# Scattering experts' results to rows of token choices, and spreading half of them by one-hot products

## The chip, the cores and the metric

One Trainium2 chip, one core. The metric is the device time of one execution in microseconds, median of the runs. TensorE is called PE, VectorE DVE, ScalarE ACT, GpSimd POOL, SyncE SP.

## What is computed

Two transformer blocks on 512 tokens of width 1024, float32 in and out. Block 1 is attention with a short convolution and an FFN of width 4096. Block 2 is a mixer and a mixture of experts (MoE), and a final norm follows. The change lies in the MoE and, with one step, in the FFN of block 1.

```python
def hierarchical_moe(h, ...):
    grp = argmax(softmax(hf @ w_group + b_group))            # 4 groups of 8 experts
    top_p, top_e = top_k(softmax(logits of the group), 2)    # two experts a token
    weights = p_grp * top_p / sum(top_p)
    ...                                                      # 1024 assignments, sorted by expert
    a = silu(xb @ w_gate[e]) * (xb @ w_up[e])                # 1024 -> 256
    out = (a @ w_down[e]) * weight                           # 256 -> 1024
    y = zeros(T, D).at[slot_tok].add(out)
x = x + gate2 * y;  return rms_norm(x, final_norm_g)
```

## The kernel before, in words

The MoE runs as 17 jobs (`Pair`), one behind the other. Jobs of pairs 0 to 15 hold two experts each with 64 slots for tokens an expert, 128 slots in all; job `NP` (16) is the overflow pair, two blocks of 64 slots for tokens that found no place, whose experts are known only at run time (`xi`). Jobs run in the order 0 to 14, `NP`, 15. A job has these steps:

- six weight panels of 1 MB (two each of gate, up, down; tile `pw`) are loaded on SP's queue into a ring of 17 places (`place`); those of `NP` are gathered on POOL's queue by `xi`;
- `gather`: an indirect DMA on POOL's queue brings the rows of up to 128 tokens from `h2d` by the table `tab` into `xg`;
- `turn`: eight transposes by PE make `xT`;
- `up` (L1898 by way of `both`): 32 pairs of products into two PSUM banks, ACT's silu and DVE's `a` (L1911);
- `turn_a`: two transposes make `aT`;
- `product` (L1898 too): 8 pairs of products of 512 columns; `scaled` (L1929) takes the two halves out of PSUM into `o`;
- `down` (L1938): POOL's queue writes all 128 rows of `o` to rows of the DRAM buffer `ye`, empty slots too.

The last job's result stays on chip: a one-hot matrix `oh` of its slots against the tokens spreads it by products (L1465). For all others, eight indirect gathers (L1490, `results`) bring for each token the two rows of `ye` that belong to it (`src`); the order of what follows is written out by hand in `TAIL`: adding the two rows (DVE L1446, POOL L1444), the residual `x` through PSUM by products with the identity (L1460), the sum (L1451), square, power, scaling (L1483) and the output. A row of zeros in `ye`, written in the FFN of block 1 (L525), serves tokens without a row.

The order of instructions on each engine is otherwise set when the kernel is built: a scheduler places each step by the estimated time at which its inputs are ready, and each engine runs its list in order. `T` is 512, `D` 1024, `P` 128, `NT` 4 tiles of tokens, `CAP` 64.

Of the kernel before, what the change touches and what calls it, by code (L numbers as in the profile page):

```python
# [29 lines left out]
YE = 30  # L30
ZERO = (YE + SX) * CAP
# [10 lines left out]
XGS = 4  # L42
# [4 lines left out]
TPOOL = (0,)  # L47
YPOOL = (1, 2)
YX = (1, 2)
XPE = (0, 1, 2, 3)  # L50
FCUT = [[slice(0, D)]] * 3 + [[slice(0, 512), slice(512, D)]]

TAIL = "d b0 b1 a0 a1 s k e0 e1 a2 t0 t1 b2 e2 b3 e3 t2 a3 f0 t3 f1 f2 f3".split()
# [13 lines left out]
def shape_constants():  # L67
# [27 lines left out]
        it(8) % 4 * P + i[:, None] - float(T),  # L95
# [9 lines left out]
class Emit:  # L105
# [410 lines left out]
    def ffn(self, x1, hh, hl, first, CH=8):  # L516
# [739 lines left out]
    def route_loads(self, mod, op):  # L1256
# [7 lines left out]
        widths = (4, 8, 32, P, 8, NX, 1, XT)  # L1264
# [76 lines left out]
    def moe(self):  # L1341
# [3 lines left out]
        with ExitStack() as c0:  # L1345
# [13 lines left out]
            with self.pool("r1", 1) as r1:  # L1359
                rest = self.route(r1, rp, tab, src, W, xb, nx, sc, kept, ws)  # L1360
            self.banks(t="y", u="zw", d="x")
            with ExitStack() as c1:
                ep = c1.enter_context(self.pool("ep", 1))
                XG = list(self.XG)

                order = list(range(NP - 1)) + [NP, NP - 1]
                jobs = [Pair(self, ep, XG[i % XGS], tab, c) for i, c in enumerate(order)]
# [7 lines left out]
                gf = self.xp.tile([P, D], F32, tag="B2", name="gf")  # L1375
                for i, j in enumerate(jobs):
                    if i > 0:
                        jobs[i - 1].turn_a()
                    if i + 1 < n:
                        jobs[i + 1].turn()  # L1380
                    if i + XGS < n:
                        jobs[i + XGS].gather()
                    if i == n - 3:

                        g1 = self.xp.tile([P, D], F32, tag="xg1", name="gf1")
                        nc.sync.dma_start(g1[0:1, :], I["final_norm_g_2"].unsqueeze(0))
                    if i == n - 2:
                        for half in range(2):
                            hs = slice(half * 512, half * 512 + 512)
                            b = self.bank("d")  # L1390
                            nc.tensor.matmul(b, self.ones[0:1, :], g1[0:1, hs], start=True, stop=True)
                            nc.scalar.copy(gf[:, hs], b)
                        oh = ep.tile([P, T], F32R, tag="oh", name="oh")
                        for tt in range(NT):
                            nc.vector.tensor_scalar(oh[:, tt * P:(tt + 1) * P], self.rt[3], kept, -float(tt * P), op0=ALU.subtract, op1=ALU.is_equal)
# [4 lines left out]
                for tt in range(NT):  # L1400
                    self.results(ys[tt], self.ye, ZERO, src[:, 0], tt)
                self.banks(t="y", u="z", d="wx")
                jobs[-1].turn_a()
                steps = self.combine(x, ys, gf, oh, jobs[-1])
                for c, f in zip("dsk", jobs[-1].last_steps(self.pin, [self.xp.tile([P, D], F32R, tag=f"xg{i}", name=self.nm("k")) for i in (2, 1)])):
                    steps[c] = f
                for c in TAIL:
                    steps[c[0]](*(int(i) for i in c[1:]))
# [4 lines left out]
                with self.tc.If(more > SX):  # L1413
                    self.yx = self.dram.tile([(NX - SX) * CAP, D], F32, tag="yx", name="yx")
                    for c in range(NP + SX // 2, NP + NX // 2):
                        xg = self.place()
                        nc.vector.memset(xg, 0.0)
                        job = Pair(self, ep, xg[:, :D], tab, c)
# [5 lines left out]
                    for tt in range(NT):  # L1424
                        y = self.wr.tile([P, 2, D], F32, tag="wr", name=self.nm("y"))
                        nc.vector.memset(y, 0.0)
                        self.results(y, self.yx, (NX - SX) * CAP - 1, src[:, 1], tt)
                        for k in range(2):
                            nc.vector.tensor_tensor(x[:, tt, :], y[:, k, :], x[:, tt, :], op=ALU.add)
                        self.finish(x, y, gf, tt, ())  # L1430
# [4 lines left out]
    def combine(self, x, ys, gf, oh, last):  # L1435

        nc, pin = self.nc, self.pin
        banks = {}
        halves = (slice(0, 512), slice(512, D))

        def add(tt):
            y = ys[tt]
            if tt in YPOOL:
                nc.gpsimd.tensor_tensor(y[:, 0, :], y[:, 0, :], y[:, 1, :], op=ALU.add)  # L1444
            else:
                pin(nc.vector.tensor_tensor(y[:, 0, :], y[:, 0, :], y[:, 1, :], op=ALU.add))  # L1446

        def total(tt):
            for half, hs in enumerate(halves):
                y = ys[tt][:, 0, hs] if tt in XPE else x[:, tt, hs]  # L1450
                pin(nc.vector.tensor_tensor(x[:, tt, hs], banks[tt, half], y, op=ALU.add))  # L1451

        def onto(tt):
            pin(nc.vector.tensor_tensor(x[:, tt, :], ys[tt][:, 0, :], x[:, tt, :], op=ALU.add))

        def begin(tt):
            for half, hs in enumerate(halves):
                b = banks[tt, half] = self.bank("tu"[half] if tt in YX else "d")
                if tt in XPE:
                    nc.tensor.matmul(b, self.ident, x[:, tt, hs], start=True, stop=False)  # L1460

        def end(tt):
            for half, hs in enumerate(halves):
                for p in range(2):
                    nc.tensor.matmul(banks[tt, half], oh[:, tt * P:(tt + 1) * P], last.kept[p][:, hs], start=tt not in XPE and p == 0, stop=p == 1)  # L1465

        return {"a": add, "t": total, "x": onto, "b": begin, "e": end,
                "f": lambda tt: self.finish(x, ys[tt], gf, tt, TPOOL, pin)}

    def finish(self, x, y, gf, tt, pool, pin=lambda i: i):  # L1470

        nc = self.nc
        xt, y = x[:, tt, :], y[:, 0, :]
        ss = self.sm.tile([P, 2], F32, tag="ss2", name=self.nm("ss"))
        nc.scalar.activation(y, xt, AF.Square, accum_out=ss[:, 0:1])
        self.rsqrt(ss[:, 1:2], ss[:, 0:1], D, 1)
        if tt in pool:
            nc.scalar.activation(y, xt, AF.Copy, scale=ss[:, 1:2])
            nc.gpsimd.tensor_tensor(y, y, gf, op=ALU.mult)
            nc.sync.dma_start(self.out[0, tt * P:(tt + 1) * P, :], y)  # L1480
        else:
            for c in FCUT[tt]:
                pin(nc.vector.scalar_tensor_tensor(y[:, c], xt[:, c], ss[:, 1:2], gf[:, c], op0=ALU.mult, op1=ALU.mult))  # L1483
                nc.sync.dma_start(self.out[0, tt * P:(tt + 1) * P, c], y[:, c])

    def results(self, y, rows, bound, src, tt):

        for k in range(2):
            i = 4 * k + tt
            self.nc.gpsimd.indirect_dma_start(out=y[:, k, :], out_offset=None, in_=rows[:, :], bounds_check=bound, oob_is_err=False,  # L1490
                                              in_offset=bass.IndirectOffsetOnAxis(ap=src[:, i:i + 1], axis=0))

    def route(self, r1, rp, tab, src, W, xb, nx, sc, kept, ws):
        nc, I = self.nc, self.I
        d4, d8, i32, iP, tokv, jx, ip, thr = self.rt
# [72 lines left out]
        def table(vr, w, o, role="b"):  # L1568
# [4 lines left out]
            return tb, beside(o, tb[C, 0:w], lambda o, v: V.tensor_scalar(o, v, float(T), None, op0=ALU.add))  # L1573
# [10 lines left out]
        tb, last = table(vm, 32, tab[:, 0:NP])  # L1584
# [4 lines left out]
        with self.tc.issue_after(last.ins):  # L1589
            beside(kept, tb[C, YE:32], lambda o, v: V.tensor_scalar(o, v, float(T), None, op0=ALU.add))  # L1590
            V.tensor_copy(cum, b[:, 0:160])

        def rest(room, room2):
# [11 lines left out]
            for o, v in ((ei, row(i32, 8)), (xi, row(xb, 8))):  # L1605
# [70 lines left out]
    def place(self):  # L1676
# [299 lines left out]
```

## Time and profile before

| what | value |
|---|---|
| median of 3 runs | 1562.48 us (1559.33 to 1566.56) |
| the profiled execution: its time, its span | 1559.03 us, 1557.1 us |
| PE busy | 1453.4 us, 93% of the span |
| DVE, ACT, POOL busy | 861.1, 568.7, 207.5 us |
| mean granted PE clock | 0.972 of full |
| last `up` ends, last DVE instruction ends | 1510.56, 1543.33 us |

Times in the trace are microseconds from the span's start. The MoE's jobs lie between 1230 and 1511 us. A wait is read in brackets behind an instruction: how long its engine had been idle, and what released it.

### The profile page before, as it was taken

How to read it: one execution, taken by the hardware profiler on the slowest of the kernel's cores; microseconds unless marked ns; L12 is line 12 of the kernel's file. 1: busy time of each engine (PE TensorE's matmuls, PEld its weight loads, DVE VectorE, ACT ScalarE, POOL GpSimd, SP SyncE). 2: the span in 40 equal slices, each digit the busy share in tenths (PEclk: the TensorE clock that was granted, in tenths of full speed). 3: DMA queues.
4: the chain of work that ended last, by engine and by line, in shares of the span. 5: the costliest groups of instructions: out<-in, count | busy, mean ns of one | idle time of the engine just before them, and what ended most of it. 6: DMA issues, size and time to landing. Idle time of an engine off the chain costs nothing.

```text
span 1557.1 us, 20093 instructions
## 1 busy us (share of the span) xinstructions
PE 1453.4 (93%) x7630; PEld 1143.4 (73%) x7630; DVE 861.1 (55%) x1836; ACT 568.7 (37%) x1198; POOL 207.5 (13%) x242
## 2 busy tenths in 40 slices
PE   7999999999999999999999999999999789887882
PEld 6877778798888888887888888888887655554441
DVE  5675887878667664468766342248756731111114
ACT  4444775743332423345443342236622211000101
POOL 2110230111011010030000110000022311010104
PEclk8999999999999999999999999999999889999996
DMA  5325102037555644433322333421167689999964
GB/s 188 101 66 179 73 28 95 1 111 242 187 167 193 210 162 135 139 120 110 109 82 55 99 127 115 135 95 55 54 212 303 265 318 414 425 425 425 426 268 163
DMA packets 131357, 275.46 MB, mean 177 GB/s; under 512 B 17870, under 2 KB 77295, under 8 KB 118200
## 3 DMA queue, kind: packets, MB, share of 16 engines
q1 hardware_dynamic: 117098, 237.66, 42.6%
q0 software_dynamic: 10704, 33.65, 5.7%
q10 hardware_dynamic: 3454, 2.82, 0.6%
q8 instruction: 62, 1.02, 0.3%
q14 instruction: 39, 0.32, 0.1%
HBM read 259.90 MB, written 18.92 MB: 179 GB/s over the span
## 4 chain that ended last, share of the span: by engine, by line
PE 64%; DMA 13%; DVE 5%; issue 5%; ACT 2%; POOL 1%; ACTq 0%; DVEq 0%; POOLq 0%; SPq 0%
PE b L157 18%; PE b L158 18%; PE b L159 18%; DMA pw<-w_expert_up 4%; DMA pw<-w_expert_down 4%; PE b L1898 3%; DMA pw<-w_expert_gate 3%; PE b L218 2%; PE b L821 1%; PE b L822 1%; DMA xg<-h2d,tab 1%; PE b L764 1%; DVE wl L151 1%; PE b L765 1%; DMA wr<-w_out 0%
## 5 line engine op out<-in xcount | busy, mean ns | idle before, releaser
L149 ACT ACTIVATE wh<-wr 128x512 fp32r<-128x512 f32 x361 | 205.3, 622 | 302.3 <-PE b L158 146.3
L151 DVE TENSOR_TENSOR wl<-wr,wh 128x512 fp32r<-128x512 f32 x349 | 235.9, 713 | 143.3 <-ACT wh L149 130.1
L1898 PE MATMUL b<-pw,xT 128*64 128x256 f32 x1088 | 139.0, 395 | 26.9 <-DMA pw<-w_expert_up 14.1
L1898 PEld LDWEIGHTS b<-pw,xT 128*64 128x64 f32 x1088 | 86.3, 141 | 76.5 <-DMA pw<-w_expert_up 17.8
L159 PE MATMUL b<-h2h,wl 128*128 128x512 f32 (+1 forms) x320 | 121.9, 381 | 0.0
L158 PE MATMUL b<-h2l,wh 128*128 128x512 f32 (+1 forms) x320 | 121.9, 381 | 0.0
L157 PE MATMUL b<-h2h,wh 128*128 128x512 f32 (+1 forms) x320 | 121.7, 381 | 0.0
L158 PE MATMUL b<-fl,wh 128*128 128x512 f32 (+1 forms) x288 | 105.2, 366 | 0.0
L157 PE MATMUL b<-fh,wh 128*128 128x512 f32 (+1 forms) x288 | 104.9, 366 | 0.2 <-ACT fh L203 0.2
L159 PE MATMUL b<-fh,wl 128*128 128x512 f32 (+1 forms) x288 | 105.1, 365 | 0.0
L157 PE MATMUL b<-wh,uh 128*128 128x512 f32 x256 | 100.0, 391 | 0.0
L159 PE MATMUL b<-wh,ul 128*128 128x512 f32 x256 | 99.7, 390 | 0.0
L158 PE MATMUL b<-wl,uh 128*128 128x512 f32 x256 | 99.6, 389 | 0.0
L498 DVE SCALAR_TENSOR_TENSOR acc<-wr,cond,acc 128x512 f32<-128x512 f32 x84 | 62.9, 748 | 36.1 <-DMA wr<-mod_w 34.4
L1911 DVE SCALAR_TENSOR_TENSOR a<-b,ws,a 128x256 f32<-128x256 f32 x17 | 8.2, 484 | 126.3 <-PE b L1898 126.3
L159 PEld LDWEIGHTS b<-h2h,wl 128*128 128x128 f32 x320 | 60.6, 189 | 11.4
L158 PEld LDWEIGHTS b<-h2l,wh 128*128 128x128 f32 x320 | 60.5, 189 | 11.3
L157 PEld LDWEIGHTS b<-h2h,wh 128*128 128x128 f32 x320 | 60.5, 190 | 11.2
L1898 PE MATMUL b<-pw,aT 128*64 128x512 f32 x272 | 67.4, 597 | 0.3 <-DMA pw<-w_expert_down 0.3
L157 PEld LDWEIGHTS b<-fh,wh 128*128 128x128 f32 x288 | 54.1, 189 | 9.7 <-ACT fh L203 0.5
L159 PEld LDWEIGHTS b<-fh,wl 128*128 128x128 f32 x288 | 54.3, 189 | 8.9
L158 PEld LDWEIGHTS b<-fl,wh 128*128 128x128 f32 x288 | 54.3, 189 | 8.8 <-DVE fl L204 0.2
(586 smaller groups left out, 3205.8 us busy)
## 6 DMA issues: line engine op xcount, KB each, us to landing
wr<-w_in SPq DMA_DIRECT2D x33, 1024.0 KB
pw<-w_expert_gate SPq DMA_DIRECT2D x32, 1024.0 KB
pw<-w_expert_up SPq DMA_DIRECT2D x32, 1024.0 KB
pw<-w_expert_down SPq DMA_DIRECT2D x32, 1024.0 KB
wr<-mod_w SPq DMA_DIRECT2D x24, 1024.0 KB
wr<-w_up SPq DMA_DIRECT2D x16, 1024.0 KB
wr<-w_down SPq DMA_DIRECT2D x16, 1024.0 KB
ye<-o POOLq DMA_DIRECT2D x16, 512.0 KB, 8.0
```

The costliest lines, as they stand in the source:

```text
L149: nc.scalar.activation(hi[:, c], raw[:, c], AF.Copy)
L151: (nc.gpsimd if i in pool else eng or nc.vector).tensor_tensor(lo[:, c], raw[:, c], hi.bitcast(F32)[:, c], op=ALU.subtract)
L157: mm(o, lh, rh, start=first, stop=False)
L158: mm(o, lh, rl, start=False, stop=False)
L159: mm(o, ll, rh, start=False, stop=last)
L218: self.nc.tensor.transpose(o, i, self.ident[:k, :k])
L498: nc.vector.scalar_tensor_tensor(acc, rv[:, k, :], self.cond[:, kk:kk + 1], acc, op0=ALU.mult, op1=ALU.add)
L764: nc.tensor.matmul(b[:, :n], QS[:, h, qs], KH[:, kind, g, :n], start=True, stop=False)
L765: nc.tensor.matmul(b[:, :n], QS[:, h, qs], KL[:, kind, g, :n], start=False, stop=True)
L821: nc.tensor.matmul(o, v, ph, start=kind == 2, stop=False)
L822: nc.tensor.matmul(o, v, pl, start=False, stop=kind == 1 and kb == qb)
L1898: self.nc.tensor.matmul(o[h, :], x[:, k, h], w[s](k), start=k == ks[0], stop=k == ks[-1])
```

## The change

Eight pairs (`HOT`: 4, 6, 8, 10, 12, 13, 14, 15) no longer write to DRAM. Their `o` is split into a high and a low part (`split`: ACT copies it to fp32r, DVE subtracts), and `spread` adds it to `x`: for each of four token tiles and two halves, two one-hot products of 128x512 into a bank of `c` and a DVE add of 128x512 onto `x`. These steps are given to a later `up` as `fill`, and stand between its products. The last two jobs (pairs 14 and 15) are added in `tail` instead, in PSUM, on top of `ident` times `x`.

The other nine ("cold") jobs write by an indirect DMA: `ye` now has a row for each token and choice (1024 rows), the table `to` says which row a slot goes to, and empty slots lie out of bounds and are not moved. Rows that no slot writes must read as zero or be skipped: four DMAs on SP's queue fill `ye` with zeros in the FFN (1 MB each), and the tile of a gather of results is set to zero first (`memset`).

The order of jobs is now 0 to 11, `NP`, 12, 13, 14, 15. All cold results are then in DRAM four jobs ahead of the end, and the gathers and adds of results stand in jobs 14 and 15 (counted from 0 in the new order), two token tiles each; DVE does all adds, two of 128x1024 a tile. `XGS` falls from 4 to 2: the buffers freed hold high and low parts. The banks of `up` fall from four to two (role `u`), `c` takes the other two. The hand-written `TAIL` order is gone; `finish` reads the sum from PSUM in halves. The routing table has two more small DVE operations ahead of the first gather.

```diff
+HOT = (4, 6, 8, 10, 12, 13, 14, 15)
+ORDER = [*range(12), NP, *range(12, NP)]
-XGS = 4
+XGS = 2
-TAIL = "d b0 b1 a0 a1 s k e0 e1 a2 t0 t1 b2 e2 b3 e3 t2 a3 f0 t3 f1 f2 f3".split()
...
-        self.ye = self.dram.tile([ZERO + 1, D], F32, tag="ye", name="ye")
-        zero = fp.tile([1, D], F32, tag="zero", name="zero")
+        self.ye = self.dram.tile([2 * T, D], F32, tag="ye", name="ye")
+        zero = fp.tile([P, 256], F32, tag="zero", name="zero")
         nc.gpsimd.memset(zero, 0.0)
-        nc.gpsimd.dma_start(self.ye[ZERO:, :], zero)
+        for i in range(4):
+            nc.sync.dma_start(self.ye[i * 256:(i + 1) * 256, :].rearrange("(p a) (b c) -> p (a b) c", p=P, c=256), zero.unsqueeze(1).to_broadcast([P, 8, 256]))
...
-            self.banks(t="y", u="zw", d="x")
+            self.banks(t="y", u="z", c="w", d="x")
...
-                    j.up()
-                    if i > 0:
-                        jobs[i - 1].down()
-                ys = [self.place().rearrange("p (k c) -> p k c", k=2) for _ in range(NT)]
-                for tt in range(NT):
-                    self.results(ys[tt], self.ye, ZERO, src[:, 0], tt)
...
+                    if i == n - 1:
+                        jobs[i - 1].down(kept)
+                    j.up(jobs[i - 2].spread(x) if hot(i - 2) else ())
+                    for tt in (2 * (i - back), 2 * (i - back) + 1):
+
+                        if 0 <= tt < NT:
+                            y = self.place().rearrange("p (k c) -> p k c", k=2)
+                            self.results(y, src[:, 0], tt)
+                            for k in range(2):
+                                nc.vector.tensor_tensor(x[:, tt, :], y[:, k, :], x[:, tt, :], op=ALU.add)
+                    if 0 < i < n - 1:
+                        jobs[i - 1].down(kept)
+                assert hot(n - 1) and hot(n - 2) and back + 1 < n
+                self.tail(x, gf, *jobs[-2:], kept)
...
+    def tail(self, x, gf, prev, last, kept):
...
+        def begin(tt, half, role):
+            b = banks[tt, half] = self.bank(role)
+            nc.tensor.matmul(b, self.ident, x[:, tt, half * 512:half * 512 + 512], start=True, stop=False)
+            prev.onto(b, tt, half, False, False)
...
+        for half in range(2):
+            for tt in range(NT):
+                last.onto(banks[tt, half], tt, half, False, True)
...
-    def results(self, y, rows, bound, src, tt):
-
+    def results(self, y, src, tt):
+
+        self.nc.vector.memset(y, 0.0)
         for k in range(2):
...
-    def down(self):
+    def down(self, kept=None):
         em = self.em
+        if kept is not None and self.c in HOT:
+            self.hot(kept)
+            for i in range(2):
+                self.scaled(self.o, i, self.product(i))
+                self.split(i)
+            return
...
-        self.nc.gpsimd.dma_start(rows[i * P:(i + 1) * P, :], o)
+        self.nc.gpsimd.indirect_dma_start(out=em.ye[:, :], out_offset=bass.IndirectOffsetOnAxis(ap=self.to[:, c:c + 1], axis=0),
+                                          in_=o, in_offset=None, bounds_check=2 * T - 1, oob_is_err=False)
...
+    def onto(self, b, tt, half, first, last):
+
+        for i, k in enumerate((self.hi, self.lo)):
+            self.nc.tensor.matmul(b, self.oh[:, tt * P:(tt + 1) * P], k[:, half * 512:half * 512 + 512], start=first and i == 0, stop=last and i == 1)
+
+    def spread(self, x):
+
+        def step(tt, half):
+            b = self.em.bank("c")
+            self.onto(b, tt, half, True, True)
+            xs = x[:, tt, half * 512:half * 512 + 512]
+            self.nc.vector.tensor_tensor(xs, b, xs, op=ALU.add)
+
+        return [lambda tt=tt, half=half: step(tt, half) for half in range(2) for tt in range(NT)]
```

Three places of the order show what moved. SP's queue at the start of the FFN of block 1, before (`wr` is a panel of weights; L492 serves the modulation of block 2, whose work is spread over the FFN):

```order
L492 DMA wr_3653<-mod_w 128x4x512
L138 DMA wr_3659<-w_up 128x8x256
L492 DMA wr_3731<-mod_w 128x4x512
L138 DMA wr_3741<-w_up 128x8x256
L492 DMA wr_3816<-mod_w 128x4x512
L492 DMA wr_3831<-mod_w 128x4x512
L138 DMA wr_3841<-w_down 128x4x512
```

and of the change:

```order
L486 DMA wr_3656<-mod_w 128x4x512
L132 DMA wr_3662<-w_up 128x8x256
L520 DMA ye<-zero 1024x1x256 x4
L486 DMA wr_3734<-mod_w 128x4x512
L132 DMA wr_3744<-w_up 128x8x256
L486 DMA wr_3819<-mod_w 128x4x512
L486 DMA wr_3834<-mod_w 128x4x512
L132 DMA wr_3844<-w_down 128x4x512
```

The four DMAs that write zeros stand ahead of two panels of the modulation and one of the FFN, and panels behind them keep their order.

POOL's queue through the last jobs, before (`xi` rows are the overflow pair's panels, `ye<-o` a job's result, `pw<-ye,src` a gather of results):

```order
L1938 DMA ye<-o_12207 128x1024
L1693 DMA pw_12258<-w_expert_up,xi 128x2048
L1693 DMA pw_12262<-w_expert_up,xi 128x2048
L1693 DMA pw_12266<-w_expert_down,xi 128x2048
L1693 DMA pw_12270<-w_expert_down,xi 128x2048
L1938 DMA ye<-o_12311 128x1024
L1938 DMA ye<-o_12379 128x1024
L1490 DMA pw_12393<-ye,src 128x1024 x2
```

and of the change, where `ye<-o_12017` is pair 9's result, `ye<-o_12241` pair 11's and `ye<-o_12327` the overflow pair's:

```order
L1932 DMA ye<-o_12017,to 1024x1024
L1864 DMA xg_10017<-h2d,tab 128x1024
L1679 DMA pw_12160<-w_expert_up,xi 128x2048
L1679 DMA pw_12164<-w_expert_down,xi 128x2048
L1679 DMA pw_12148<-w_expert_gate,xi 128x2048
L1679 DMA pw_12168<-w_expert_down,xi 128x2048
L1932 DMA ye<-o_12241,to 1024x1024
L1864 DMA xg_10018<-h2d,tab 128x1024
L1864 DMA xg_10017<-h2d,tab 128x1024
L1932 DMA ye<-o_12327,to 1024x1024
L1475 DMA pw_12425<-ye,src 128x1024 x2
L1475 DMA pw_12574<-ye,src 128x1024 x2
```

The overflow pair's panels now stand two cold results ahead of its own, and the gathers of results stand behind that last scatter with nothing else in between, two for each token tile (those of the last two tiles follow).

DVE's list of the change in jobs 13 to 15 (`a_12412` is `a` of job 14, `a_12561` of job 15; `o_12435` and `k_12437` are pair 12's result and its low part, `o_12584` and `k_12586` pair 13's; `x<-pw` adds a gathered row onto `x`, `x<-b` a spread):

```order
L1472 MEMSET pw_12425 128x2048
L1918 TENSOR_TENSOR o_12435<-b_12443,S_10003 128x512
L198 TENSOR_TENSOR k_12437<-o_12435,k_12436 128x512
L1397 TENSOR_TENSOR x_10000<-pw_12425,x_10000 128x1024
L1918 TENSOR_TENSOR o_12435<-b_12451,S_10003 128x512
L1397 TENSOR_TENSOR x_10000<-pw_12425,x_10000 128x1024
L198 TENSOR_TENSOR k_12437<-o_12435,k_12436 128x512
L1472 MEMSET pw_12574 128x2048
L1472 MEMSET pw_12415 128x2048
L1900 SCALAR_TENSOR_TENSOR a_12412<-b_12395,ws,a_12412 128x256
L1963 TENSOR_TENSOR x_10000<-b_12506,x_10000 128x512
L1877 COPY xT_12464<-b_12471 128x512
```

and further on, at job 15:

```order
L198 TENSOR_TENSOR k_12586<-o_12584,k_12585 128x512
L1397 TENSOR_TENSOR x_10000<-pw_12574,x_10000 128x1024
L1472 MEMSET pw_12564 128x2048
L1900 SCALAR_TENSOR_TENSOR a_12561<-b_12528,ws,a_12561 128x256
L1397 TENSOR_TENSOR x_10000<-pw_12574,x_10000 128x1024
L1918 TENSOR_TENSOR o_12584<-b_12600,S_10003 128x512
L1946 TENSOR_SCALAR oh_12615<-rt,kept 128x128 x4
L198 TENSOR_TENSOR k_12586<-o_12584,k_12585 128x512
L1397 TENSOR_TENSOR x_10000<-pw_12564,x_10000 128x1024
L1918 TENSOR_TENSOR o_12613<-b_12620,S_10003 128x512
```

In before, none of this stood between `o` and `a`: all adds of gathered rows came behind the last `a`. Now the two adds of the first token tile and the memsets for the next two stand ahead of `a` of job 14, and the adds and memset of later tiles on both sides of `a` of job 15.

## Rows read from the trace of the kernel before

**Rows 1.** The page: busy time of PE; GB/s in 40 slices of the span.

```profile
PE 1453.4 (93%) x7630; PEld 1143.4 (73%) x7630; DVE 861.1 (55%) x1836; ACT 568.7 (37%) x1198; POOL 207.5 (13%) x242
...
GB/s 188 101 66 179 73 28 95 1 111 242 187 167 193 210 162 135 139 120 110 109 82 55 99 127 115 135 95 55 54 212 303 265 318 414 425 425 425 426 268 163
```

**Rows 2.** Stretches of the MoE: us, busy by engine (x), PEclk, DMA share, GB/s.

```profile
1270.00:1340.00 70.00, 69.69 (x519) 40.84 (x516) 14.17 (x22) 7.08 (x16) 9.17 (x12) 1.00 1.01 408
1340.00:1490.00 150.00, 116.98 (x766) 67.52 (x763) 20.94 (x33) 12.28 (x27) 15.87 (x19) 0.96 1.01 425
```

**Rows 3.** Timeline of DVE, 1265 to 1512, ends of `up`: start, us, operation.

```profile
1312.43 0.48 DVE L1911 SCALAR_TENSOR_TENSOR a<-b,ws,a 128x256 f32<-128x256 f32 x1 [6.45 <-PE b L1898]
...
1324.59 0.48 DVE L1911 SCALAR_TENSOR_TENSOR a<-b,ws,a 128x256 f32<-128x256 f32 x1 [6.45 <-PE b L1898]
...
1441.04 0.48 DVE L1911 SCALAR_TENSOR_TENSOR a<-b,ws,a 128x256 f32<-128x256 f32 x1 [8.68 <-PE b L1898]
...
1463.06 0.48 DVE L1911 SCALAR_TENSOR_TENSOR a<-b,ws,a 128x256 f32<-128x256 f32 x1 [13.19 <-PE b L1898]
...
1510.56 0.48 DVE L1911 SCALAR_TENSOR_TENSOR a<-b,ws,a 128x256 f32<-128x256 f32 x1 [3.26 <-PE b L1898]
```

**Rows 4.** Timeline of all engines, 1459 to 1474: one job's turns and product.

```profile
1463.60 0.51 PE L218 MATMUL b<-ident,a 128*128 128x128 f32 x2 [0.65 <-DVE a L1911]
...
1464.20 0.37 ACT L1920 COPY aT<-b 128x256 f32<-128x256 f32 x1 [7.01 <-PE b L218]
...
1465.27 3.70 PE L1898 MATMUL b<-pw,aT 128*64 128x512 f32 x16
```

**Rows 5.** Timeline of all engines, 343 to 349 (FFN).

```profile
343.31 0.37 SPq L138 DMA_DIRECT2D wr<-w_up  x1
...
348.54 0.63 ACT L149 ACTIVATE wh<-wr 128x512 fp32r<-128x512 f32 x1 [1.92 <-DMA wr<-w_up]
```

**Rows 6.** Stretches of the FFN, columns as in rows 2.

```profile
350.00:360.00 10.00, 10.00 (x45) 8.28 (x45) 8.50 (x13) 3.60 (x7) 1.07 (x1) 1.00 0.77 257
370.00:400.00 30.00, 30.00 (x133) 24.37 (x133) 20.75 (x32) 7.18 (x14) 2.78 (x4) 1.00 0.66 215
```

**Rows 7.** Groups of 1180 to 1557: busy us, mean ns, idle before.

```profile
L1451 DVE TENSOR_TENSOR x<-b,pw 128x512 f32<-128x512 f32 x8 | 5.1, 685 | 2.1 <-PE b L1465 2.0
...
L1951 DVE TENSOR_TENSOR k<-o,k 128x512 fp32r<-128x512 f32 x2 | 1.3, 688 | 0.1
```

**Rows 8.** Timeline of all engines, 1469 to 1492: panels of the overflow pair.

```profile
1470.90 1.04 POOL L1693 DMA_INDIRECT pw<-w_expert_up,xi  x1 [0.34 <-PE b L1391]
...
1489.11 1.12 PE L1898 MATMUL b<-pw,xT 128*64 128x256 f32 x4 [4.22 <-DMA pw<-w_expert_up,xi]
```

**Rows 9.** Timeline of all engines, 1500 to 1545: the tail.

```profile
1512.81 0.55 POOL L1938 DMA_DIRECT2D ye<-o  x1 [12.02 <-DVE o L1929]
...
1516.59 3.70 PE L1460 MATMUL b<-x,ident 128*128 128x512 f32 x8
1516.60 1.03 POOL L1490 DMA_INDIRECT pw<-ye,src  x1 [3.24 <-DMA ye<-o]
...
1517.94 1.03 POOL L1490 DMA_INDIRECT pw<-ye,src  x1 [0.30 <-issue]
...
1523.29 1.23 DVE L1446 TENSOR_TENSOR pw<-pw 128x1024 f32<-128x1024 f32 x1 [10.78 <-DMA pw<-ye,src]
1524.43 1.28 DVE L1929 TENSOR_TENSOR o<-b,S 128x512 f32<-128x512 f32 x2
...
1540.72 2.61 DVE L1483 SCALAR_TENSOR_TENSOR pw<-x,ss,gf 128x1024 f32<-128x1024 f32 x3 [0.55 <-POOL ss L214]
```

**Rows 10.** DMA issues of 1230 to 1557: KB each, median us to landing.

```profile
ye<-o POOLq DMA_DIRECT2D x16, 512.0 KB, 8.0
...
pw<-ye,src POOLq DMA_INDIRECT x8, 6.4
```

More of the change, by code (lines that the diff above doesn't have):

```diff
@@ L1375, in moe @@
                 gf = self.xp.tile([P, D], F32, tag="B2", name="gf")
+                hot = lambda i: i >= 0 and jobs[i].c in HOT
+                back = max(i for i in range(n) if not hot(i)) + 2
                 for i, j in enumerate(jobs):
@@ L1432, in pin @@
     def pin(self, i):
         return self.tc.keep_in_program_order(i)
-    def combine(self, x, ys, gf, oh, last):
-        nc, pin = self.nc, self.pin
+    def tail(self, x, gf, prev, last, kept):
+        nc = self.nc
         banks = {}
[L1439 to L1468, printed above, removed]
@@ L1486, in results @@
-    def results(self, y, rows, bound, src, tt):
+        def begin(tt, half, role):
+            b = banks[tt, half] = self.bank(role)
+            nc.tensor.matmul(b, self.ident, x[:, tt, half * 512:half * 512 + 512], start=True, stop=False)
+            prev.onto(b, tt, half, False, False)
+        last.turn_a()
+        for tt, role in ((0, "c"), (1, "u")):
+            for half in range(2):
+                begin(tt, half, role)
+        products = [last.product(i) for i in range(2)]
+        for half in range(2):
+            begin(2, half, "t")
@@ new lines, in tail @@
+        last.hot(kept)
+        for half in range(2):
+            last.scaled(last.o, half, products[half])
+            last.split(half)
+        for half in range(2):
+            begin(3, half, "d")
+        for half in range(2):
+            for tt in range(NT):
+                last.onto(banks[tt, half], tt, half, False, True)
+        for tt in range(NT):
+            self.finish(gf, tt, [banks[tt, half] for half in range(2)], self.place()[:, :D])
+        for tt, half in sorted(banks):
+            nc.scalar.copy(x[:, tt, half * 512:half * 512 + 512], banks[tt, half])
@@ L1583, in route @@
             tt_(oc[:, hs], row(iC, 4), bc(pos[:, hs], CAP), ALU.is_equal)
-        tb, last = table(vm, 32, tab[:, 0:NP])
+        rows, last = table(vm, 32, slice(0, NP))
         warm = self.bank()
@@ new lines, in hot @@
+    def hot(self, kept):
+        em, nc = self.em, self.nc
+        self.o = self.tl("o", D)
+        if self.c in ORDER[-2:]:
+            k = em.place(F32R)
+            self.hi, self.lo = k[:, :D], k[:, D:]
+        else:
+            self.hi, self.lo = (em.xp.tile([P, D], F32R, tag=f"xg{i}", name=em.nm("k")) for i in (2, 3))
+        self.oh = self.tl("oh", T, dt=F32R)
+        for tt in range(NT):
+            nc.vector.tensor_scalar(self.oh[:, tt * P:(tt + 1) * P], em.rt[3], kept[:, self.c:self.c + 1], -float(tt * P), op0=ALU.subtract, op1=ALU.is_equal)
```

145 lines of the change are left out of this document (58 added, 87 removed).

## Prediction

> **What bounds the kernel now.** I read the page first, then stretches, then single jobs. The page [rows 1] has PE busy for 93% of the span, which is an average over two regimes: the GB/s line climbs to 425 and stays there for the last fifth. The stretches [rows 2] divide that fifth. From 1270 to 1340 us PE is busy 69.69 of 70 us, so PE sets the pace although the DMA engines are full too. From 1340 to 1490 PE is busy 116.98 of 150 and the DMA share is 1.01 at 425 GB/s: weight panels set the pace. The reader is to see a prefetch that is used up by 1340. The end of each `up` [rows 3] gives the pace of a job: 12.16 us (1312.43 to 1324.59) where PE is the bound, (1441.04 − 1324.59)/7 = 16.6 us where panels are. The last `up` ends at 1510.56, the last DVE instruction at 1543.33, the span at 1557.1: 13.8 us of output and closing lie behind it. The profiled run took 1559.03 us, 3.45 below the median of the three, 1562.48. My sum is made against 1557.1 and 3.45 + 1.93 is added to it.
>
> **One job, in prices.** In [rows 4], counted from DVE's `a` at 1463.06 [rows 3]: `turn_a` and `turn` run 1463.60 to 1465.27, the product 3.70 more, to 1468.97. That leaves 12.16 − 1.67 − 3.70 = 6.79 us for `up`. Where the product stands ahead of the next `up`, PE can do nothing while `a` and its transposed copy (0.37) are made, and a job takes 5.91 + 0.37 + 6.79 = 13.1 us.
>
> **What the change does, part by part.**
>
> *Bytes.* Sixteen writes of 512 KB go, 8.39 MB, of which fourteen (7.3 MB) were issued while the DMA engines were full. Nine scatters take their place. Counting the fixed inputs' routing, pairs 0, 1, 2, 3, 5, 7, 9 and 11 hold 444 filled slots and the two overflow blocks 41; 485 rows of 4 KB are 1.99 MB. The gathers of results (again 1.99 MB, empty sources are skipped) move from the free DMA engines at the end into the full stretch. That is 7.3 − 4.0 = 3.3 MB less, at 425 GB/s 7.8 us of panel time.
>
> *Zeroing.* Four DMAs of 1 MB write zeros on SP's ring at the start of the FFN, ahead of a mod_w and of the w_up issued at 343.31 [rows 5]. From 350 to 360 the engines moved 257 GB/s at share 0.77 [rows 6], 334 GB/s at share 1, so 4.19 MB take 12.6 us, from about 333 to 346. ACT already waited 1.92 us for that w_up, until 348.54; it will land near 354.5 and the w_down behind it is late too. PE was full (10.00 of 10, 30.00 of 30) on what had been prepared. Between nothing (all of the 6 us absorbed) and 10 us (two panels late, nothing absorbed) I take 5 us, lost by PE. The two further DVE operations in the routing table ahead of the first gather cost 0.4 us.
>
> *Hot pairs on PE.* Each of eight adds 16 products of 128x512 in fp32r. In the FFN 133 of that shape took 30 us of a full PE [rows 6], 0.226 each, so 3.63 us. The low part of the result (0.69 [rows 7]; ACT makes the high part beside it) is ahead of the first of them, and the eight adds of DVE, 0.685 each [rows 7], follow over two banks, in groups of four: 0.7 for the split and about 2 us of bank waits. I take 6.4 us where a spread lies inside an `up`, bounds 3.6 (all hidden) and 8 (DVE's 5.5 plus splits bare).
>
> *Jobs 6 to 12.* Spreads of pairs 4, 6, 8 and 10 lie in the `up`s of jobs 6, 8, 10, 12: 7 × 13.1 + 4 × 6.4 = 117.3 us of PE. Panels alone need 7 × 6.8 MB / 425 GB/s = 112, scatters 2 more, and start with the credit above. So PE is now the bound there and the stretch takes about 117, as long as the 116.5 that panels set before. The saved bytes buy nothing in it. Job 5 ends at 1324.6 + 5.4 = 1330, job 12 at 1447, and job 13, which has no product ahead of it, 9.4 later: 1456.5.
>
> *NP moved from place 15 to 12.* In before its six panels were issued late on POOL behind a `ye` write (the first up,xi at 1470.90) and PE waited 4.22 us for the second, until 1489.11 [rows 8], 18 us behind that issue. In the new POOL queue the last of them stand behind the scatter of pair 9, two jobs ahead of need, about 32 us: no wait, already counted.
>
> *Results added by DVE between jobs 13 and 16.* This decides. Before, gathers were issued at 1516.60, 3.8 us behind the last `ye` write, and DVE's add began at 1523.29, 5.35 behind its second gather [rows 9]; DVE had waited 10.78 us, and the two `o` operations behind it, whose products PE finished by 1516.7, came only after. Now the adds stand in DVE's queue ahead of `a` of job 14, ahead of `o` of pair 13 and, the third block, ahead of `o` of pair 14; each pair of gathers is issued only behind a memset that DVE runs after the block before. The memset of 128x2048 has no row: below nothing, above four passes of 128x512, 2.7 us; I take 2.7, the nearest row of that engine.
> Counting from job 13's `a` (t): PE alone needs product 3.7, turns 2.2, product 3.7, the broadcast of the norm weight 1.9 (an estimate: four products, half of the eight in [rows 9]), `up` 6.8: 18.3. On DVE: scatter issued t + 4.5, landed 3.8 to 8.0 later [rows 9, 10], two gathers 1.3 apart landing 5.35 to 6.4 after the second [rows 10]: t + 15 to 20; add 1.23, split 0.69, two memsets 5.4: `a` of job 14 at t + 25 (22 to 28). Job 15: PE alone 2.2 + 3.7 + 6.8 + 3.6 + 1 of bank waits = 17.3; DVE gets through its adds 9 us after `a`, PE stops at the fifth spread step, whose bank waits for DVE, and 19.5 results. Job 16: PE alone 16.5 (no second `turn`); gathers issued at `a`, added 9.5 us later, then `o`, split and two spread adds, to 12, then the rest of `up` and the spreads: 22. Together 66.5 instead of 52.
> The Trainium skill bears on this: "TensorE: Matmul & The Clock Gate", section "Architectural detail: the array is 16× 32×32, not 1× 128×128", says that ACT and DVE are strict FIFO, so a waiting add holds all behind it. By that rule the sum is the one with 66.5; the late `o` at 1524 in the trace agrees with it. Its page "VectorE: DVE Perf Modes", section "Zero memsets can be issued as uint32 (trn2)", gives one cycle per element; for 2048 elements I estimate 2.1 us from that page, which would take 1.2 us from job 14 and 0.6 from job 15; no row here shows it.
>
> *Tail.* Gone: the wait for gathers and GpSimd's adds (of 33 us from last `a` to last DVE). Left: eight ident products (3.70 for eight [rows 9]), 32 one-hot products 7.3, the pair's product 3.7, turn, `o`, split, then squares from PSUM, power, two scalings per token tile. About 18.5 on PE and 6.5 behind it: 25 us, 8 less.
>
> Sum: 1456.5 + 66.5 + 25 + 13.8 = 1561.8, against 1557.1. With 5.4 around it that is **1567** against the median 1562.5, 0.3% more; within 0.5% is about what a measurement of this kernel can't tell from no change.
>
> **Rivals.**
> - *The waits stay hidden* (gathers land sooner, or PE has other work for the time): 52 instead of 66.5, span 1547, with no loss at the zeroing 1542; 1547 to 1553 on the median's scale. For it: after 1470 less is queued on the DMA engines than before. Against it: `a` of job 14 stands behind two adds in DVE's queue, and a write plus a gather can't be faster than the 10.5 us from 1512.81 to 1523.29 in [rows 9]. It needs the wait at `a` under 3 us.
> - *Zero writes are slow.* Pieces of 1 KB from 128 rows, at half the read rate: 25 us, w_up 18 late, PE loses 12 to 15 instead of 5: 1575 to 1578, slower. It decides from about 9 us of PE loss. For it: PE's stock there is unknown; against: the FFN's engines were half idle.
> - *Scatters block.* Indirect writes land in 12 to 16 us instead of 8; each is in POOL's queue ahead of the next job's row gather, and the last holds the first results: 1572 to 1585. The nearest rows are the direct write (8.0) and the indirect gather (6.4) [rows 10], neither of them a scatter.
> - *It does nothing in the middle and all is decided at the end by panels:* last panels landing near 1500 leave the last `up` at 1508 at the earliest; that is the first rival's end, not below it.
>
> **How the numbers follow.** The forecast has 0.42 (own range 1558 to 1576), hidden waits 0.32, slow zeroing 0.14, slow scatters 0.12. The first gives most of "same" and some of "slower", hidden waits nearly all of "faster": faster 0.34, same 0.28, slower 0.38. The range goes from the hidden waits without the best of it, 1545, to the slow cases without the worst, 1582.
>
> **What would show it.** Right: PE full in the middle jobs, and DMA share under 1 there; waits of DVE for `pw<-ye,src` three times of 4 to 8 us between jobs 13 and 16, with PE waiting for DVE; 12 us of full DMA at 333 to 346 and ACT waiting for w_up. Wrong: last `up` ending before 1512 (hidden waits), PE idle over 8 us in the FFN (zeroing), PE waiting for panels in the middle, or a tail over 28 us.

## The result, and the profile after

The changed kernel took 1571.82 us (median of 14 runs, 1567.12 to 1581.12), the kernel before in the same session 1561.39 (14 runs): a ratio of 1.0065, interval 1.0048 to 1.0083. The forecast was 1567 against 1562.5, a ratio of 1.003. It is slower by 0.65%, just beyond the 0.5% that the prediction called no change.

The page of the changed kernel, the lines that answer to [rows 1]:

```profile
PE 1481.2 (94%) x7742; PEld 1157.4 (74%) x7742; DVE 914.0 (58%) x1938; ACT 583.1 (37%) x1227; POOL 198.3 (13%) x231
...
GB/s 186 98 67 180 69 28 93 3 177 227 212 161 198 197 194 113 143 134 86 131 82 54 96 121 121 134 94 55 54 233 285 309 315 403 425 424 425 405 110 55
```

PE is busy 28 us longer, and its share rose. The plateau of 425 GB/s falls to 405 in the last slice but two, where it was 426, and the last two slices hold 110 and 55 GB/s instead of 268 and 163: the results no longer travel at the end.

Stretches of the MoE of the changed kernel, columns as in [rows 2]:

```profile
1330.00:1400.00 70.00, 66.99 (x398) 36.80 (x394) 31.50 (x55) 9.07 (x18) 6.06 (x6) 1.00 1.01 425
1400.00:1461.00 61.00, 55.89 (x394) 34.08 (x395) 17.82 (x35) 6.64 (x14) 12.15 (x12) 1.00 1.01 424
1461.00:1536.00 75.00, 58.89 (x316) 29.97 (x313) 38.75 (x52) 8.30 (x16) 8.98 (x9) 0.91 0.58 229
```

Up to 1461 PE is nearly full while the DMA engines still move 425 GB/s. Then, with the DMA share at 0.58, PE is busy 58.89 of 75 us. In that stretch neither PE nor the DMA engines are full, and its mean granted clock is 0.91.

DVE's timeline of the changed kernel from `a` of job 13 to `a` of job 16 (L1900 is `a`, L1397 the add of a gathered row, L1472 the memset):

```profile
1460.98 0.48 DVE L1900 SCALAR_TENSOR_TENSOR a<-b,ws,a 128x256 f32<-128x256 f32 x1 [6.00 <-PE b L1886]
...
1467.07 1.76 DVE L1472 MEMSET pw<- 128x2048 f32 x1 [0.38 <-DMA pw<-w_expert_gate]
...
1482.09 1.23 DVE L1397 TENSOR_TENSOR x<-pw,x 128x1024 f32<-128x1024 f32 x1 [11.31 <-DMA pw<-ye,src]
...
1485.31 1.23 DVE L1397 TENSOR_TENSOR x<-pw,x 128x1024 f32<-128x1024 f32 x1 [1.39 <-DMA pw<-ye,src]
...
1487.51 1.76 DVE L1472 MEMSET pw<- 128x2048 f32 x1 [0.38 <-DVE k L198]
1489.65 1.76 DVE L1472 MEMSET pw<- 128x2048 f32 x1 [0.38 <-issue]
1491.33 0.36 DVE L1900 SCALAR_TENSOR_TENSOR a<-b,ws,a 128x256 f32<-128x256 f32 x1
...
1499.36 1.23 DVE L1397 TENSOR_TENSOR x<-pw,x 128x1024 f32<-128x1024 f32 x1 [3.62 <-DMA pw<-ye,src]
...
1511.20 1.76 DVE L1472 MEMSET pw<- 128x2048 f32 x1 [0.37 <-issue]
1513.05 0.48 DVE L1900 SCALAR_TENSOR_TENSOR a<-b,ws,a 128x256 f32<-128x256 f32 x1
...
1535.97 0.48 DVE L1900 SCALAR_TENSOR_TENSOR a<-b,ws,a 128x256 f32<-128x256 f32 x1
```

The add at 1482.09 waited 11.31 us for its gather, and `a` of job 14 stands behind two adds and two memsets, at 1491.33. PE had done the products of that `up` at 1479. What DVE waited for was issued on POOL's timeline (L1932 scatters the overflow pair's result, L1475 gathers):

```profile
1465.31 1.01 POOL L1932 DMA_INDIRECT ye<-o,to  x1 [9.78 <-DVE o L1918]
1474.20 1.02 POOL L1475 DMA_INDIRECT pw<-ye,src  x1 [7.88 <-issue]
1475.52 1.00 POOL L1475 DMA_INDIRECT pw<-ye,src  x1 [0.30 <-issue]
1490.02 0.99 POOL L1475 DMA_INDIRECT pw<-ye,src  x1 [13.49 <-issue]
...
1513.24 0.99 POOL L1475 DMA_INDIRECT pw<-ye,src  x1 [18.34 <-DVE pw L1472]
```

The scatter was issued 4.33 us behind `a` of job 13, the first gather 8.89 behind the scatter, and the add of its rows began 7.89 later. The gathers at 1490.02 and 1513.24 follow within 0.8 us on the end of a memset of DVE.

ACT and PE at the same time show how far the wait of DVE reaches:

```profile
1483.95 0.63 ACT L197 ACTIVATE k<-o 128x512 fp32r<-128x512 f32 x1 [8.79 <-DVE o L1918]
1484.48 0.57 ACT L1387 COPY gf<-b 128x512 f32<-128x512 f32 x1
```

```profile
1475.32 3.67 PE L1886 MATMUL b<-pw,xT 128*64 128x256 f32 x30
...
1485.11 1.22 PE L1955 MATMUL b<-k,oh 128*128 128x512 f32 x2 [5.45 <-ACT gf L1387]
1491.75 0.70 PE L212 MATMUL b<-ident,a 128*128 128x128 f32 x2 [5.42 <-DVE a L1900]
1492.24 1.91 PE L212 MATMUL b<-ident,xg 128*128 128x128 f32 x8
```

ACT stood 8.79 us for `o`, which DVE had behind the waiting add. Behind that split stood ACT's copy of the norm weight out of the bank (L1387), and PE waited 5.45 us for the copy to give the bank free, then 5.42 for `a`. The eight transposes at 1492.24 took 1.91 us; in [rows 4] two and eight of them together took 1.67. After the stall PE runs slower for a while, at a mean granted clock of 0.76:

```profile
1490.00:1500.00 10.00, 8.08 (x30) 4.00 (x30) 4.32 (x6) 0.96 (x2) 3.97 (x4) 0.76 0.79 302
```

By landmarks, in us (`w_o` is the third of the four loads of `w_o` on SP's queue in block 1, ahead of the FFN):

| stage | before | after | forecast | difference to before |
|---|---|---|---|---|
| start to `w_o` | 196.98 | 203.30 | 196.98 | +6.32 |
| `w_o` to `a` of job 0 | 1070.07 | 1069.56 | 1075.5 | −0.51 |
| job 0 to 5 | 57.54 | 57.54 | 57.5 | 0 |
| job 5 to 13 | 138.47 | 130.58 | 126.5 | −7.89 |
| job 13 to 16 | 47.50 | 74.99 | 66.5 | +27.49 |
| job 16 to the span's end | 46.54 | 35.53 | 38.8 | −11.01 |

The first line belongs to the one profiled execution and not to the change: up to the zeros in the FFN each engine has the same instructions in the same order in both kernels. One wait of DVE between 150 and 205 us, before and in the changed kernel:

```profile
DVE p L768 <- DMA base<-k_dist: 3.3, 1, 3.3
```

```profile
DVE p L763 <- DMA base<-k_dist: 6.2, 1, 6.2
```

It is the wait for one small table of distances, and its 2.9 us more are about half of the 6.32; the rest was not followed. In the nine other profiles of this study `w_o` lies between 196.9 and 201.2. So the profiled spans differ by 14.4 us, of which 8.1 lie behind that landmark, and the medians differ by 10.4.

### The profile page after: what moved, and what is told of

It reads as the page before. It is cut to its first block, busy times and chain, and to the rows that moved or that the text cites. A ratio compares the mean times of both kernels' runs of the same rounds, so it can differ in the third digit from the quotient of the medians.

```text
span 1571.5 us, 20447 instructions
## 1 busy us (share of the span) xinstructions
PE 1481.2 (94%) x7742; PEld 1157.4 (74%) x7742; DVE 914.0 (58%) x1938; ACT 583.1 (37%) x1227; POOL 198.3 (13%) x231
## 3 DMA queue, kind: packets, MB, share of 16 engines
q0 software_dynamic: 9664, 25.04, 4.4%
## 5 line engine op out<-in xcount | busy, mean ns | idle before, releaser
L1886 PE MATMUL b<-pw,xT 128*64 128x256 f32 x1088 | 134.4, 386 | 1.4 <-DMA pw<-w_expert_gate,xi 1.4
L492 DVE SCALAR_TENSOR_TENSOR acc<-wr,cond,acc 128x512 f32<-128x512 f32 x84 | 62.9, 749 | 37.2 <-DMA wr<-mod_w 35.5
L152 PEld LDWEIGHTS b<-wl,uh 128*128 128x128 f32 x256 | 48.1, 188 | 11.5 <-DVE wl L145 1.5
```

The costliest lines, as they stand in the source:

```text
L152: mm(o, lh, rl, start=False, stop=False)
L492: nc.vector.scalar_tensor_tensor(acc, rv[:, k, :], self.cond[:, kk:kk + 1], acc, op0=ALU.mult, op1=ALU.add)
L1886: self.nc.tensor.matmul(o[h, :], x[:, k, h], w[s](k), start=k == ks[0], stop=k == ks[-1])
```

## The experiments

Ratios are to the kernel before, run on the same chip at the same time. Stages are from `a` of one job to `a` of another, as in the table.

**The adds behind the last `up`.** In the loop only memset and gathers stay:

```diff
-                            for k in range(2):
-                                nc.vector.tensor_tensor(x[:, tt, :], y[:, k, :], x[:, tt, :], op=ALU.add)
+                            ys.append(y)
...
+                for tt, y in enumerate(ys):
+                    for k in range(2):
+                        nc.vector.tensor_tensor(x[:, tt, :], y[:, k, :], x[:, tt, :], op=ALU.add)
                 self.tail(x, gf, *jobs[-2:], kept)
```

> The changed kernel, with the gathers of results and their memsets where they are, but the eight adds of gathered rows written behind the last up, so that DVE's list has them behind a of job 15. Theory (DVE stands still for gathered rows with work of PE queued behind it): from job 13's a to job 16's a 57 to 62 us instead of 75, no wait of DVE for gathered rows over 1 us, run 12 to 18 us shorter than the changed kernel's 1572, so 1554 to 1560. Rival (spreads and products of PE alone fill the time, the waits only lie beside them): 70 to 75 us there and a run within 4 us of the changed kernel's. Rival (gathers land late whoever waits): the wait of 8 to 11 us reappears ahead of a of job 16 or in the tail, run 1566 to 1572.

Measured: 1551.8 us, ratio 0.9947 (0.9930 to 0.9965), 1.2% less than the changed kernel's ratio. `a` of jobs 13 to 16 on DVE's timeline, and the whole stretch from the first to the last:

```profile
1458.27 0.48 DVE L1903 SCALAR_TENSOR_TENSOR a<-b,ws,a 128x256 f32<-128x256 f32 x1 [6.00 <-PE b L1889]
...
1476.32 0.48 DVE L1903 SCALAR_TENSOR_TENSOR a<-b,ws,a 128x256 f32<-128x256 f32 x1
...
1498.23 0.48 DVE L1903 SCALAR_TENSOR_TENSOR a<-b,ws,a 128x256 f32<-128x256 f32 x1 [1.58 <-PE b L1889]
...
1516.90 0.48 DVE L1903 SCALAR_TENSOR_TENSOR a<-b,ws,a 128x256 f32<-128x256 f32 x1 [3.54 <-PE b L1889]
```

```profile
1458.27:1516.90 58.63, 57.50 (x325) 30.18 (x321) 39.39 (x55) 8.25 (x16) 10.54 (x9) 1.00 0.72 297
```

Job 13 to 16 takes 58.63 us instead of 74.99. No add waits for a gather any more, and PE is busy 57.50 of 58.63, at full clock. Gathers and adds are the same in number and size: where the adds stand in DVE's list is worth 16 us here. The run is 2 us below the 1554 to 1560 expected; the kernel before was also 2.5 us faster in that session (1558.9).

**Zeros written twice.**

```diff
-        for i in range(4):
+        for i in (0, 1, 2, 3, 0, 1, 2, 3):
             nc.sync.dma_start(self.ye[i * 256:(i + 1) * 256, :]...
```

> The changed kernel with the four zeroing DMAs issued twice (8.4 MB instead of 4.2). Prediction's step (zeroing costs PE 5 us): the second set costs at least as much as the first, 5 to 12 us, run 1577 to 1584, PE idle in the FFN doubled. Rival (the zeros lie beside work that PE has in stock; what the two profiles differ by ahead of the FFN is chance): PE loses under 4 us between 330 and 420, run within 4 us of 1572.

Measured: 1581.6 us, ratio 1.0147 (1.0120 to 1.0174). The second set cost what the prediction's step said, the first what the rival said. From `w_o` to `a` of job 0 this kernel takes 1082.2 us; with one set 1069.0 to 1073.4 (seven profiles: the changed kernel and six of this section), without 1069.5 and 1070.1 (the kernel before and the fourth experiment). The first set costs between nothing and 4 us, the second 9 to 13. The changed kernel's FFN, and that with two sets (stretches, then a wait of PE):

```profile
340.00:350.00 10.00, 10.00 (x85) 10.00 (x85) 8.54 (x16) 4.92 (x9) 0.83 (x2) 1.00 1.02 361
370.00:400.00 30.00, 26.91 (x118) 21.23 (x117) 23.58 (x38) 8.98 (x16) 4.80 (x6) 1.00 0.68 228
```

```profile
330.00:350.00 20.00, 19.75 (x148) 18.64 (x147) 11.99 (x20) 7.96 (x15) 1.62 (x3) 1.00 0.91 319
350.00:370.00 20.00, 11.43 (x42) 8.26 (x41) 9.23 (x13) 5.16 (x9) 1.28 (x1) 0.75 0.87 307
```

```profile
PE b L504 <- ACT ac L497: 8.4, 1, 8.4
```

While zeros are written the engines are full, at 361 GB/s. With one set PE loses 3 us of 370 to 400, and `a` of job 0 shows nothing of it. With two, the modulation's panel behind them is so late that PE waits 8.4 us for the sum made from it (L504), in order, with the FFN's products behind it, and the mean clock of that stretch falls to 0.75.

**Fewer pairs spread.**

```diff
-HOT = (4, 6, 8, 10, 12, 13, 14, 15)
+HOT = (12, 13, 14, 15)
```

> The changed kernel with only the last four jobs' pairs (12 to 15) spread by products; pairs 4, 6, 8 and 10 are scattered too. Theory (in jobs 6 to 12 PE is the bound, 7.4 us for each spread): the stretch from a of job 5 to a of job 12 falls from 121.4 us to what the DMA engines need, 112 to 116, run 5 to 9 us shorter than the changed kernel. Rival (the DMA engines set that pace anyway): stretch 120 to 123, run the same or up to 4 us longer for 212 more rows scattered and gathered.

Measured: 1576.36 us, ratio 1.0114 (1.0092 to 1.0137), behind the changed kernel. My theory fell. From job 5 to 12 it takes 125.12 us instead of 121.44, a little over what the rival said (120 to 123):

```profile
1343.00:1400.00 57.00, 48.26 (x322) 28.81 (x324) 9.76 (x15) 4.99 (x11) 10.08 (x10) 0.97 1.01 424
1400.00:1451.00 51.00, 36.61 (x222) 20.34 (x218) 5.12 (x8) 3.07 (x7) 8.06 (x8) 0.90 1.01 425
```

The DMA engines are full at 425 GB/s and PE is busy 36.61 of 51: without the four middle spreads panels are the bound. In the changed kernel, then, both bounds lie within some 4 us of each other. The loss against the changed kernel is 0.49%, 7.6 us, and nearly twice what the rival allowed: 3.7 us arise from job 5 to 13, 3.0 from 13 to 16 (78.0 us) and 1 behind it.

**The kernel before, its overflow pair moved alone.**

```diff
-                order = list(range(NP - 1)) + [NP, NP - 1]
+                order = [*range(12), NP, *range(12, NP)]
```

> The kernel before with its overflow pair at place 12 instead of 15 and nothing else changed. Theory A (the DMA engines are full to 1490 us whatever waits for whom, so the order of panels changes which job waits): PE's waits for the overflow pair's panels (7.0 us) go or move, the last a within 3 us, run within 0.3% of before. Theory B (those 7 us are lost by the late issue on POOL alone): run 5 to 7 us shorter, 0.3 to 0.45%.

Measured: 1552.51 us, ratio 0.9950 (0.9930 to 0.9970). The time is theory B's. The waits of PE from 1260 to 1560 us are not:

```profile
PE b L1898 <- DMA pw<-w_expert_up: 9.3, 4, 2.9
...
PE b L1898 <- DMA pw<-w_expert_up,xi: 4.9, 1, 4.9
PE b L1898 <- DMA pw<-w_expert_gate,xi: 1.5, 1, 1.5
```

The panels of the overflow pair (`xi`) still cost PE 6.4 us of the 7.0. All its waits for panels together fell from 27.2 to 21.0 us, so what went is mostly waits for other panels; why is not shown. From job 5 to 13 it takes 135.1 us (138.5 before), from 13 to the end 90.2 (94.0). This one line gives 0.5% alone (0.3 to 0.7); the change, which contains it, lost 0.65%, so the rest of the change on top of it cost about 1.2%.

**Late adds with six pairs spread.**

```diff
-HOT = (4, 6, 8, 10, 12, 13, 14, 15)
+HOT = (6, 10, 12, 13, 14, 15)
```

> The kernel with late adds, and pairs 4 and 8 scattered instead of spread (pairs 6, 10 and 12 to 15 spread). Theory (two bounds close together: PE with four spreads in the middle, panels with none; two spreads balance them): PE loses 7.4 us less for each spread taken out and waits 3 to 6 us for panels instead; from a of job 5 to a of job 13 126 to 130 us instead of 130.6, run 1548 to 1552, 0.2% faster than with all eight at best. Rival (panels set the pace as soon as one spread goes, since each cold pair adds bytes): stretch over 131, run 1552 to 1558.

Measured: 1548.7 us, ratio 0.9931 (0.9900 to 0.9962). Job 5 to 13 takes 127.64 us, 2.9 less than with eight. PE's largest wait for panels:

```profile
PE b L1889 <- DMA pw<-w_expert_up: 4.3, 2, 3.5
```

Jobs 6 and 9, now without a spread, are 4.0 and 7.5 us shorter, but job 10 is 7.4 longer: PE waits 4.3 us there for these panels, and the granted clock falls to 0.92. The run beats both kernels and has the lowest ratio here. Against the late adds with eight pairs (0.9947) the intervals overlap; the stage says more than the total.

**Late adds with four pairs spread**, the edit of the third experiment on top of the first:

> The kernel with late adds and only pairs 12 to 15 spread. Theory (the loss of 7 us by which the run with four hot pairs was behind the changed kernel is panel time in jobs 6 to 13, independent of the adds at the end): stretch from a of job 5 to a of job 13 134 us as in that run, from job 13 to 16 57 to 60 us, run 1556 to 1561, 5 to 8 us behind all eight. Rival (it came from the end, where more rows are gathered): stretch 130, run 1550 to 1553.

Measured: 1557.13 us, ratio 0.9970 (0.9946 to 0.9993). Job 5 to 13 takes 134.19 us, 13 to 16 58.66. The loss of 3.6 us in the middle is the same with early and with late adds, as the theory said. But that is all of it here (0.23%, not the 5 to 8 us expected): the other half of what the third experiment lost arose at the end and went with the early adds. The intervals with four and with eight pairs overlap, so it is again the stage that says this.

**Gathers and adds one job later.**

```diff
-                back = max(i for i in range(n) if not hot(i)) + 2
+                back = max(i for i in range(n) if not hot(i)) + 3
```

> The changed kernel with the gathers of results and their adds one job later (jobs 15 and 16 instead of 14 and 15), so that the first gather no longer waits for the scatter of the overflow pair just ahead. Theory (the first and longest wait, 11 us, is scatter plus gather landing one behind the other with DVE waiting; later ones are a gather alone, issued only when DVE gets to its memset): from a of job 13 to a of job 14 18 to 20 us instead of 30; the waits for the later tiles stay, 3 to 8 us each, one of them now in the tail; run 1558 to 1565. Rival (any wait for gathered rows costs the same wherever it stands): run 1567 to 1573.

Measured: 1558.55 us, ratio 0.9986 (0.9968 to 1.0004). DVE's timeline:

```profile
1458.22 0.48 DVE L1900 SCALAR_TENSOR_TENSOR a<-b,ws,a 128x256 f32<-128x256 f32 x1 [6.00 <-PE b L1886]
1459.08 1.76 DVE L1472 MEMSET pw<- 128x2048 f32 x1 [0.38 <-DMA pw<-w_expert_down]
...
1476.27 0.48 DVE L1900 SCALAR_TENSOR_TENSOR a<-b,ws,a 128x256 f32<-128x256 f32 x1 [3.43 <-PE b L1886]
...
1484.75 1.22 DVE L1397 TENSOR_TENSOR x<-pw,x 128x1024 f32<-128x1024 f32 x1
...
1502.06 1.23 DVE L1397 TENSOR_TENSOR x<-pw,x 128x1024 f32<-128x1024 f32 x1 [4.60 <-DMA pw<-ye,src]
...
1525.40 2.48 DVE L1397 TENSOR_TENSOR x<-pw,x 128x1024 f32<-128x1024 f32 x2 [2.23 <-DMA pw<-ye,src]
```

The first memset now runs right behind `a` of job 13, its gather lands while PE works, and its add (1484.75) waits for nothing. Job 13 to 14 takes 18.05 us instead of 30.35. Two waits for later tiles remain, 4.60 and 2.23 us. A wait costs by where it stands: moving the first one took 12 us away, where moving all of them took 16.

**Late adds with GpSimd's memsets.**

```diff
-        self.nc.vector.memset(y, 0.0)
+        self.nc.gpsimd.memset(y, 0.0)
```

> The kernel with late adds, and the four memsets of 128x2048 done by GpSimd instead of DVE (7 us of DVE's time). Theory (with late adds PE is the bound at the end, DVE only where a spread's bank waits for it): run within 3 us of the late adds alone, 1549 to 1553, from a of job 13 to a of job 16 56 to 59 us. Rival (DVE's own work is now the bound there): 5 us shorter, 1545 to 1548. Rival (GpSimd's memset is slow enough to hold up the gathers behind it): waits for gathered rows come back, 1555 to 1562.

Measured: 1552.46 us, ratio 0.9947 (0.9930 to 0.9964), the same as late adds alone; job 13 to 16 takes 59.49 us (56 to 59 expected). POOL's row of the first:

```profile
1461.59 1.83 POOL L1475 MEMSET pw<- 128x2048 f32 x1
```

GpSimd's memset takes 1.83 us, DVE's 1.76, and neither rival came: DVE is not the bound once the adds are late.

## Why the prediction was right, and where its terms were off

**The sign and the place.** The step that was to decide did: DVE waits for gathered rows with `a` and `o` behind them. Late adds take 16 of the 27 us away, and the time falls below that of before. The rule of the Trainium skill ("TensorE: Matmul & The Clock Gate", section "Architectural detail: the array is 16× 32×32, not 1× 128×128") that DVE and ACT take their work in strict order agrees with the trace: `a`, whose products were done at 1479, ran at 1491.33, and ACT's copy stood behind a split that waited 8.79 us.

**The total and the signs.** That the total came out close (8.1 us more behind `w_o`, forecast 4.7) is in part luck: the stages were off by −5.9 (`w_o` to job 0), +4.1, +8.5 and −3.3 us, and these errors mostly cancel. Of the signs named, PE full in the middle came (66.99 of 70); a DMA share under 1 there did not (1.01); DVE's waits for gathered rows were 11.31, 1.39 and 3.62 us instead of three of 4 to 8; zeros kept the engines full for 12 us (share 1.02 from 340 to 352), but ACT's wait for `w_up` was 0.35 us.

**Job 13 to 16: 75.0 for 66.5.** The mechanism was right and its sizes were off: job 14 took 30.35 us for 25 (bounds 22 to 28), job 15 21.72 for 19.5, job 16 22.92 for 22. The scatter landed 8.15 us behind its issue, and the gather was issued 8.89 behind it, over the bound of 8.0. The adds of the two rows began 7.89 and 9.79 us behind their gathers' issues, not 5.35 to 6.4; those came from the end of before (DMA share 0.66 from 1516 to 1524), while here the DMA engines are still full (0.98 from 1474 to 1486). The memset takes 1.76 us and not 2.7; the 2.1 estimated from the Trainium skill's "VectorE: DVE Perf Modes", section "Zero memsets can be issued as uint32 (trn2)", was the better price, if a little high. And the clock after a stall was left out: PE is busy 58.9 us in the stretch, against 57.5 with late adds, though nine more products lie in the latter (325 records for 316). Six of these are one-hot products and three products with the identity; at 0.23 and 0.46 us each [rows 6, 9] they are 2.7 us, so I estimate the clock's price at 4 us.

**Zeroing: 0 to 4 for 5.** The step that had 5 us "lost by PE" failed: with one set PE loses some 3 us from 370 to 400, and nothing of it is left at `a` of job 0. That the second set costs 9 to 13 us, in one profile, suggests that the first about uses up what PE has in stock. The profile seems to confirm the 5: `a` of job 0 lies 5.81 us later. But those us had arisen ahead of the FFN, by chance, and the landmark tells them apart.

**Job 5 to 13: 130.6 for 126.5.** PE does set the pace, with the DMA engines full beside it. The spreads stand in jobs 6, 7, 9 and 11, not 6, 8, 10 and 12, which leaves the sum as it is. Jobs 7, 9 and 11 took 20.1 to 20.5 us and a job without a spread 12.9, so a spread cost 7.2 to 7.6 there and not 6.4. Job 6 took 20.08; without a spread it takes 16.05 (with four and with six pairs spread; 16.06 before), because the results' products of two jobs lie in it, which the 13.1 for each job did not have. There the spread added 4.0. One-hot products of one job, most of the sixteen, on PE's timeline of the changed kernel:

```profile
1358.55 1.20 PE L1955 MATMUL b<-k,oh 128*128 128x512 f32 x4
1359.67 3.67 PE L1886 MATMUL b<-pw,xT 128*64 128x256 f32 x32
1363.28 1.20 PE L1955 MATMUL b<-k,oh 128*128 128x512 f32 x4
1364.88 1.25 PE L1955 MATMUL b<-k,oh 128*128 128x512 f32 x4 [0.41 <-DVE x L1963]
1366.37 0.50 PE L1955 MATMUL b<-k,oh 128*128 128x512 f32 x1 [0.24 <-DVE x L1963]
```

Four products take 1.12 us until the next product starts (1358.55 to 1359.67), 0.28 each and not 0.226, and waits of 0.41 and 0.24 for DVE's adds follow. PE also waited 1.4 us for a gate panel of the overflow pair, which the prediction had as none. Its panel time of 114 us for the stretch was too low, as the runs without the middle spreads show: 125 from job 5 to 12, of which some 2 are an estimate for the 212 more rows that they scatter, at 425 GB/s. So the two bounds were closer than it said; that did not change the sum, only what taking spreads out would do.

**Overflow pair's move.** It was counted as no more than a wait that goes. It is worth 0.5% alone (1552.5 us), and the prediction had no term that separates it from the rest.

**Tail: 35.5 for 38.8.** The products and scalings took 24.5 us as forecast (25); the closing is 11.0 and not 13.8; the last outputs go out in smaller pieces, but whether that is the cause was not tried.

The rivals: hidden waits did not come. Slow zeroing did not come: the engines moved 350 GB/s from 340 to 352, and only a second set cost 9 us or more. Slow scatters did not come where the first results hang on them: five of the changed kernel's nine have a landing in the trace, 7.8 to 9.3 us behind their issue, not 12 to 16. In the run with the gathers a job later one in the middle took 15.31. The first rival's price nearly held: with the waits gone the ratio is 0.9947, 1554 on the prediction's scale, where it said 1547 to 1553.

## What to carry to other kernels

Before placing work on an engine that runs its list in order, ask what stands behind it in that list: in this kernel an add that waits for a transfer belongs behind everything that the bound engine needs, even if its result seems due sooner. When a change has several parts, run the smallest alone; here one line of order gave 0.5%, and the whole change with late adds, which contains that line, shows nothing clear of noise beyond it (0.9947 and 0.9931 against 0.9950, with intervals that overlap). Compare two profiles from landmark to landmark, as a chance wait early in one execution moves all that follows.

## What was not expected of the hardware

- A stall of PE cost more than its length: after waits of 5.45 and 5.42 us the granted clock was 0.76 from 1490 to 1500 and 0.91 from 1461 to 1536, a mean of its full and its half level, and PE's work there took some 4 us longer than with late adds at 1.00 (the estimate above). With zeros written twice one wait of 8.4 us left 0.75 for the stretch 350 to 370.
- The changed kernel's indirect scatters landed a median of 8.3 us behind their issue (five of nine have it in the trace), the last one 8.15 with the DMA engines near full, about as long as the direct writes of all 128 rows (8.0 [rows 10]). Leaving the empty rows out saved bytes (with the gathers of results, POOL's queue moved 25.04 MB instead of 33.65) and no latency.
- Zeroing 128x2048 costs DVE 1.76 us and GpSimd 1.83, so here it may stand on whichever waits less.
